# Block attention in half as many TensorE blocks: four heads' scores into four banks, four heads' outputs into one, transposes a piece later

## The chip, the cores and the metric

One core of one Trainium2 chip runs the whole program. The metric is device time in microseconds (us) of that core: the kernel before has a median of 471.4 us over 3 runs (471.27 to 472.64).

## What is computed

A decoder block on 256 tokens of width 1024, all in float32. Three token mixers run on the same normed input: block attention (8 heads of 64), retention (4 heads of 128) and attention on a memory of 256 tokens (4 heads of 128). Their outputs are gated and added, and a feed-forward part with a short convolution follows. With 256 tokens there is a single block of 256, so the block attention is plain causal attention with a relative bias:

```
s_own = einsum('bhqd,bhnd->bhqn', q_c, k_own) * dh**-0.5 + table[:, rel_bucket(d_own)]
s_own = where(d_own >= 0, s_own, NEG_INF)
p     = softmax(s_own)
y     = einsum('bhqn,bhne->bhqe', p, v_own)
```

## The kernel before

All weights stream through in 150 **pieces** of 128x1024. For piece q, SyncE has loaded the raw weights, ScalarE rounds them to a high part `whi` (L141) and VectorE subtracts to get the low part `wlo` (L142); both are made three pieces ahead of their use (`LA = 3`). TensorE then multiplies the piece. A `proj_a` piece is 24 matmuls of 256 columns at L183, a `proj_b` piece is 12 of 512 columns at L170 to L172. A `proj_a` piece goes through its eight k in an order (function `unit`) whose last two matmuls read the low part of the activations for k = 6 and k = 7.

Everything that is not a projection hangs in the gaps between pieces. `at(p, fn, ...)` puts a step on a list, and `tick()` issues the steps of piece p right behind the matmuls of piece p, in the order in which they were listed. Nothing reorders them afterwards: each engine runs its instructions in the order of issue.

The block attention has these steps, at pieces counted from 16:

- `moba_s`: scores. One call takes the two heads that share one 128-partition slice of `qa` and `ka` (64 partitions each), writes them to the two `sps` banks (L370), and has VectorE add the bias and take the two row maxima for both heads (L373, L376).
- `moba_e`: exponentials and row sums on ScalarE (L383).
- `moba_n`: reciprocal and scaling on VectorE (L389, L391).
- `moba_t`: three transposes on TensorE into a `tps` bank (L395 to L397), copied out by ScalarE (L398).
- `moba_v`: outputs of two heads (L409), into one half of the single `yps` bank.
- `moba_y`: rounding and splitting of a full `yps` bank into `ya` (`split_to`: ScalarE L156, VectorE L157), once for every four heads.

For the pair f the scores are issued at piece 16 + 3f, `moba_e` one and two pieces later for its two heads, `moba_n` two and three, `moba_t` three and four, `moba_v` five. Each step is written as one float32 matmul in the source and is two instructions on TensorE.

Other work in the same gaps: the second normed input `nm` (the memory) is split into high and low parts by `Norm.split` at pieces 16 to 19, two k for each piece (`gained`: ScalarE L214, VectorE L215), and is read by the projections of pieces 20 to 27. The projections of pieces 16 to 19 are evacuated into `qm` (L156, L157), those of pieces 20 to 23 into `km`, of 24 to 27 into `vm`, and from piece 28 the retention's `qr` and `kr` are made with rotary products on VectorE (L505, L507). The memory attention starts at piece 30 with the same kinds of banks: `mem_s` (L443) takes an `sps` bank at pieces 30, 33, 36 and 39, `mem_t` (L470) a `tps` bank three pieces later, and `mem_v` (L480) the `yps` bank from piece 34 on.

Of the eight accumulator banks, three are `mm` (projections), two `sps`, two `tps` and one `yps`. All small SBUF tiles (`w2`) share eight buffers.

Of the kernel before, what the change touches and what calls it, by code (L numbers as in the profile page):

```python
# [25 lines left out]
FT = mybir.dt.float32  # L26
FR = mybir.dt.float32r
AF = mybir.ActivationFunctionType
OP = mybir.AluOpType
AX = mybir.AxisListType  # L30

P = 128
D = 1024
T = 256
# [22 lines left out]
def block_kernel(ctx, tc, w, xt, mt, par, cst, onehot, relb, gng, gfin, out):  # L57
    nc = tc.nc
# [4 lines left out]
    act = pool("act")  # L63
# [10 lines left out]
    def s_ps():  # L74
        return psp.tile([P, 512], FT, name="sps", bufs=2)

    def t_ps():
        return psp.tile([P, 512], FT, name="tps", bufs=2)

    def y_ps():  # L80
        return psp.tile([P, 512], FT, name="yps", bufs=1)
# [10 lines left out]
    def w2():  # L92
        return act.tile([P, 512], FT, name="w2", bufs=8)

    def qk_tile():
        return mix.tile([P, 4, T], FT, name="qk", bufs=2)

    def v_tile():
        return mix.tile([P, 2, 512], FT, name="vv", bufs=2)
# [16 lines left out]
    def at(p, fn, *args):  # L116

        works[p].append((fn, args))
# [146 lines left out]
    for k in range(KD):  # L265
        if k < 2 or k % 2 == 0:
            a = 8 + T * k if k else 0
            b = 8 + T * (k + 1 if k < 2 else k + 2)
            nc.sync.dma_start(xs[:, a:b], xt[:, a:b])
        wk, a = (w0, w1)[k // 4], 512 * (k % 4)  # L270
# [55 lines left out]
    hank = mix.tile([P, 8, 384], FT, name="hank")  # L326
# [22 lines left out]
    qa, ka, va = qk_tile(), qk_tile(), v_tile()  # L349
# [9 lines left out]
    asc = 64 ** -0.5  # L359
    mo = {}  # L360
    halves = ((1, slice(0, 256)), (0, slice(256, 384)))

    def moba_s(f):


        sps = [s_ps(), s_ps()]
        for q, k, o in ((slice(128, 256), 256, 0), (slice(0, 128), 128, 256)):
            for hh in range(2):
                pp = slice(64 * hh, 64 * hh + 64)
                nc.tensor.matmul(sps[hh][:, o:o + k], qa[pp, f, q], ka[pp, f, :k], start=True, stop=True)  # L370
        for hh in range(2):
            h, sp, sb = 2 * f + hh, sps[hh], w2()
            nc.vector.scalar_tensor_tensor(sb[:, :384], sp[:, :384], asc, hank[:, h, ::-1], op0=OP.mult, op1=OP.add)  # L373
            mx = act.tile([P, 2], FT, name="amx", bufs=2)
            for t, s in halves:
                nc.vector.tensor_reduce(out=mx[:, t:t + 1], in_=sb[:, s], axis=AX.X, op=OP.max, negate=True)  # L376
            mo["p", h] = sb, mx

    def moba_e(h):
        sb, mx = mo["p", h]  # L380
# [17 lines left out]
        nc.scalar.copy(pt[:, :384], tp[:, :384])  # L398
        mo["t", h] = pt

    def moba_v(f):
        if f % 2 == 0:
            mo["y"] = y_ps()
        o = T * (f % 2)
        for j, a in enumerate((0, 128)):
            for hh in range(2):
                h = 2 * f + hh
                src = mo["t", h][:, 0:256] if j == 0 else mo["t", h][:, 256:384]
                nc.tensor.matmul(mo["y"][64 * hh:64 * hh + 64, o + a:o + 256], va[:, j, 64 * h:64 * h + 64],  # L409
                                 src, start=(j == 0), stop=(j == 1))  # L410

    def moba_y(i):
        split_to(ya, slice(2 * i, 2 * i + 2), kt(mo["y"]))

    for f in range(4):
        b = 16 + 3 * f
        at(b + 5, moba_v, f)
        if f % 2 == 1:
            at(b + 6, moba_y, f // 2)
        at(b, moba_s, f)  # L420
        for hh in range(2):
            at(b + hh + 3, moba_t, 2 * f + hh)
            at(b + hh + 2, moba_n, 2 * f + hh)
            at(b + hh + 1, moba_e, 2 * f + hh)


    qm, km = yt_tile(), yt_tile()
# [58 lines left out]
    for h in range(4):  # L486
        b = 30 + 3 * h
# [147 lines left out]
    for u in range(4):  # L635
        ps = proj_a(mh, 2)
        s = slice(2 * u, 2 * u + 2)
# [51 lines left out]
    for f in range(NF):  # L689
        ps = proj_a(hg if f < DEFER else nh.out)  # L690
        p = count["used"]
        if f < DEFER:
# [4 lines left out]
            p = U0 + 7 + 10 * f  # L697
# [184 lines left out]
```

## Time and profile before

| | |
|---|---|
| median of 3 runs | 471.4 us (471.27 to 472.64) |
| profiled execution | 471.54 us, its span 469.8 us |
| TensorE matmuls busy | 460.1 us, 98% of the span |
| TensorE weight loads busy | 435.7 us, 93% |
| VectorE busy | 348.7 us, 74% |
| ScalarE busy | 258.1 us, 55% |
| GpSimd busy | 61.8 us, 13% |
| DMA | 86.75 MB, mean 185 GB/s |
| mean granted TensorE clock | 0.997 of full speed |

The span runs from the first to the last instruction of the program. Matmuls are pipelined, so one that is said to take 0.28 us is followed by the next after less than half of that; steps from start to start tell more than durations. The block attention lies between 58.9 us and 109.9 us of the span.

### The profile page before, as it was taken

The page shows a single profiled execution, that of the slowest core. Times are in us where ns is not written, and L with a number is a line of the kernel's source. Part 1 is how long each engine was busy: PE and PEld are TensorE (multiplying, and loading weights), DVE is VectorE, ACT ScalarE, POOL GpSimd, SP SyncE. Part 2 cuts the span into 40 slices and gives each one's busy share as a digit, 9 for nine tenths or more (in the row PEclk, how much of TensorE's full clock was granted, in tenths as well). Part 3 has the DMA queues.
Part 4 walks back from the last instruction along what each step waited for, and adds up shares of the span by engine and source line. Part 5 has one row for each costly group of instructions (what it writes and reads, how often), then busy time and mean ns, then how long its engine had stood idle before and what let it go on. Part 6 is the DMA issues. An engine that isn't in the chain of part 4 may idle for free.

```text
span 469.8 us, 8509 instructions
## 1 busy us (share of the span) xinstructions
PE 460.1 (98%) x3470; PEld 435.7 (93%) x3470; DVE 348.7 (74%) x536; ACT 258.1 (55%) x412; POOL 61.8 (13%) x47
## 2 busy tenths in 40 slices
PE   8999999999999999999999999999999999999994
PEld 6899889889989999999999999999999999888883
DVE  5969798768976567776677779989879899744433
ACT  5747575555447434344455656767667676533323
POOL 3354510003210022321000005000000000000003
PEclk9999999999999999999999999999999999999998
DMA  8989744443554445444554574655555545655102
GB/s 259 403 347 309 248 134 162 153 158 134 177 182 140 153 160 179 148 170 166 191 215 145 191 291 161 246 190 176 183 179 180 181 181 179 191 193 196 48 1 89
DMA packets 16342, 86.75 MB, mean 185 GB/s; under 512 B 1672, under 2 KB 4272, under 8 KB 6832
## 3 DMA queue, kind: packets, MB, share of 16 engines
q1 hardware_dynamic: 16016, 85.70, 51.4%
q8 instruction: 27, 0.44, 0.4%
q10 hardware_dynamic: 288, 0.52, 0.3%
q14 instruction: 11, 0.09, 0.1%
HBM read 85.15 MB, written 1.06 MB: 184 GB/s over the span
## 4 chain that ended last, share of the span: by engine, by line
PE 91%; DVE 3%; DMA 1%; issue 1%; SPq 1%; ACT 1%; POOL 0%; POOLq 0%; ACTq 0%; DVEq 0%
PE mm L183 65%; PE mm L172 3%; PE mm L170 3%; PE mm L171 3%; PE tps L710 2%; PE tps L711 2%; PE tps L712 2%; PE sps L710 1%; PE sps L711 1%; PE sps L712 1%; DVE wlo L142 1%; DMA raw<-in_w 1%; DVE act L215 1%; PE yps L409 1%; PE sps L443 1%
## 5 line engine op out<-in xcount | busy, mean ns | idle before, releaser
L183 PE MATMUL mm<-act,whi 128*128 128x256 f32 x1600 | 291.7, 282 | 0.0
L183 PEld LDWEIGHTS mm<-act,whi 128*128 128x128 f32 x1600 | 247.9, 188 | 1.5 <-issue 1.0
L142 DVE TENSOR_TENSOR wlo<-raw,whi 128x1024 fp32r<-128x1024 f32 (+1 forms) x154 | 196.2, 1278 | 65.9 <-ACT whi L141 65.7
L141 ACT CAST whi<-raw 128x1024 fp32r<-128x1024 f32 (+1 forms) x154 | 157.7, 1026 | 123.9 <-PE mm L183 74.5
L183 PE MATMUL mm<-act,wlo 128*128 128x256 f32 x800 | 215.4, 280 | 0.0
L183 PEld LDWEIGHTS mm<-act,wlo 128*128 128x128 f32 x800 | 150.6, 188 | 0.0
L678 DVE SCALAR_TENSOR_TENSOR w<-mm,pr,w 128x255 f32<-128x255 f32 (+1 forms) x72 | 29.8, 478 | 10.2 <-ACT w L673 10.2
L183 PE MATMUL mm<-yt,whi 128*128 128x256 f32 x192 | 36.6, 282 | 0.0
L183 PEld LDWEIGHTS mm<-yt,whi 128*128 128x128 f32 x192 | 30.4, 188 | 0.0
L673 ACT ACTIVATE w<-mm,pr 128x256 f32<-128x256 f32 x36 | 18.4, 560 | 16.3 <-PE mm L183 16.2
L170 PE MATMUL mm<-whi,act 128*128 128x512 f32 x64 | 26.6, 415 | 0.7 <-ACT whi L141 0.7
L172 PE MATMUL mm<-wlo,act 128*128 128x512 f32 x64 | 26.1, 408 | 0.6 <-DVE wlo L142 0.5
L171 PE MATMUL mm<-whi,act 128*128 128x512 f32 x64 | 25.9, 404 | 0.0
L183 PE MATMUL mm<-yt,wlo 128*128 128x256 f32 x96 | 25.1, 282 | 0.0
L739 POOL TENSOR_TENSOR hN<-hN,gfb 128x512 f32<-128x512 f32 x2 | 2.6, 1280 | 169.8 <-ACT w L735 169.8
L183 PEld LDWEIGHTS mm<-yt,wlo 128*128 128x128 f32 x96 | 18.1, 188 | 0.0
L710 PE MATMUL tps<-whi,ah 128*128 128x512 f32 x44 | 17.5, 397 | 0.0
L509 POOL TENSOR_TENSOR qk<-qk,w 128x512 f32<-128x512 f32 x4 | 9.3, 2314 | 62.3 <-DVE w L507 62.3
L711 PE MATMUL tps<-whi,ah 128*128 128x512 f32 x44 | 17.4, 396 | 0.0
L712 PE MATMUL tps<-wlo,ah 128*128 128x512 f32 x44 | 17.3, 393 | 0.0
L172 PEld LDWEIGHTS mm<-wlo,act 128*128 128x128 f32 x64 | 12.3, 192 | 5.2 <-DVE wlo L142 2.5
L170 PEld LDWEIGHTS mm<-whi,act 128*128 128x128 f32 x64 | 12.4, 194 | 3.6 <-ACT whi L141 1.0
(160 smaller groups left out, 504.3 us busy)
## 6 DMA issues: line engine op xcount, KB each, us to landing
raw<-in_w SPq DMA_DIRECT2D x72, 1024.0 KB, 4.9
raw<-in_w SPq DMA_DIRECT2D x8, 256.0 KB, 5.9
raw<-in_w SPq DMA_DIRECT2D x2, 512.0 KB, 6.2
big<-in_mt SPq DMA_DIRECT2D x1, 1024.0 KB
hank<-rel_d SPq DMA_DIRECT2D x1, 1024.0 KB, 12.4
raw<-in_xt SPq DMA_DIRECT2D x1, 1024.0 KB, 4.8
ct<-in_cst SPq DMA_DIRECT2D x1, 770.0 KB, 4.6
big<-in_xt SPq DMA_DIRECT2D x3, 256.0 KB, 5.9
```

The costliest lines, as they stand in the source:

```text
L141: nc.scalar.copy(hi[:, a:b], r)
L142: nc.vector.tensor_tensor(out=lo[:, a:b], in0=r, in1=hi[:, a:b].bitcast(FT), op=OP.subtract)
L170: nc.tensor.matmul(ps[t], xh, wh, start=(k == 0), stop=False)
L171: nc.tensor.matmul(ps[t], xl, wh, start=False, stop=False)
L172: nc.tensor.matmul(ps[t], xh, wl, start=False, stop=(k == KD - 1))
L183: nc.tensor.matmul(p, wk, src[:, b, k], start=(i == 0), stop=(i == len(order) - 1))
L509: nc.gpsimd.tensor_tensor(out=d, in0=d, in1=tmp, op=OP.add)
L673: nc.scalar.activation(ac[:, i], ps[:, i], AF.Identity, bias=pr[:, CONV_B + c:CONV_B + c + 1], scale=cw(2, c))
L678: nc.vector.scalar_tensor_tensor(ac[:, i, s:], ps[:, i, :T - s], cw(2 - s, c), ac[:, i, s:], op0=OP.mult, op1=OP.add)
L710: nc.tensor.matmul(p, xh, hi[:, a:b], start=(f == 0), stop=False)
L711: nc.tensor.matmul(p, xl, hi[:, a:b], start=False, stop=False)
L712: nc.tensor.matmul(p, xh, lo[:, a:b], start=False, stop=(f == NF - 1))
```

## The change

The scores are taken four heads at a time. `moba_s(i)` writes four banks, the two `sps` and the two `tps`, and holds matmuls only; the bias and the maxima become a step of their own for each head, `moba_b`, issued at four pieces one after the other. Outputs are also taken four heads at a time, so `moba_v(i)` fills the whole `yps` bank in one go. There are two calls of each in place of four, at pieces 16 and 24 (scores) and 24 and 32 (outputs). The transposes of a head are issued two pieces behind its `moba_n`, where they were one behind. The buffers `amx` of the maxima go from two to four.

```diff
-    def moba_s(f):
-        sps = [s_ps(), s_ps()]
-        for q, k, o in ((slice(128, 256), 256, 0), (slice(0, 128), 128, 256)):
-            for hh in range(2):
-                pp = slice(64 * hh, 64 * hh + 64)
-                nc.tensor.matmul(sps[hh][:, o:o + k], qa[pp, f, q], ka[pp, f, :k], start=True, stop=True)
-        for hh in range(2):
-            h, sp, sb = 2 * f + hh, sps[hh], w2()
-            nc.vector.scalar_tensor_tensor(sb[:, :384], sp[:, :384], asc, hank[:, h, ::-1], op0=OP.mult, op1=OP.add)
-            mx = act.tile([P, 2], FT, name="amx", bufs=2)
-            for t, s in halves:
-                nc.vector.tensor_reduce(out=mx[:, t:t + 1], in_=sb[:, s], axis=AX.X, op=OP.max, negate=True)
-            mo["p", h] = sb, mx
+    def moba_s(i):
+        mo["s"] = sps = [s_ps(), s_ps(), t_ps(), t_ps()]
+        for f in range(2):
+            for q, k, o in ((slice(128, 256), 256, 0), (slice(0, 128), 128, 256)):
+                for hh in range(2):
+                    pp = slice(64 * hh, 64 * hh + 64)
+                    nc.tensor.matmul(sps[2 * f + hh][:, o:o + k], qa[pp, 2 * i + f, q], ka[pp, 2 * i + f, :k],
+                                     start=True, stop=True)
+
+    def moba_b(h):
+        sp, sb = mo["s"][h % 4], w2()
+        nc.vector.scalar_tensor_tensor(sb[:, :384], sp[:, :384], asc, hank[:, h, ::-1], op0=OP.mult, op1=OP.add)
+        mx = act.tile([P, 2], FT, name="amx", bufs=4)
+        for t, s in halves:
+            nc.vector.tensor_reduce(out=mx[:, t:t + 1], in_=sb[:, s], axis=AX.X, op=OP.max, negate=True)
+        mo["p", h] = sb, mx
...
-    def moba_v(f):
-        if f % 2 == 0:
-            mo["y"] = y_ps()
-        o = T * (f % 2)
-        for j, a in enumerate((0, 128)):
-            for hh in range(2):
-                h = 2 * f + hh
-                ...
+    def moba_v(i):
+        mo["y"] = y_ps()
+        for f in range(2):
+            o = T * f
+            for j, a in enumerate((0, 128)):
+                for hh in range(2):
+                    h = 4 * i + 2 * f + hh
+                    ...
...
-    for f in range(4):
-        b = 16 + 3 * f
-        at(b + 5, moba_v, f)
-        if f % 2 == 1:
-            at(b + 6, moba_y, f // 2)
-        at(b, moba_s, f)
-        for hh in range(2):
-            at(b + hh + 3, moba_t, 2 * f + hh)
-            at(b + hh + 2, moba_n, 2 * f + hh)
-            at(b + hh + 1, moba_e, 2 * f + hh)
+    for i in range(2):
+        b = 16 + 8 * i
+        at(b, moba_s, i)
+        at(b + 8, moba_v, i)
+        at(b + 9, moba_y, i)
+        for j in range(4):
+            at(b + 4 + j, moba_t, 4 * i + j)
+            at(b + 2 + j, moba_n, 4 * i + j)
+            at(b + 1 + j, moba_e, 4 * i + j)
+            at(b + j, moba_b, 4 * i + j)
```

## Rows read from the trace of the kernel before

**Rows 1.** The page: busy time by engine, and the granted TensorE clock in 40 slices.

```profile
PE 460.1 (98%) x3470; PEld 435.7 (93%) x3470; DVE 348.7 (74%) x536; ACT 258.1 (55%) x412; POOL 61.8 (13%) x47
...
PEclk9999999999999999999999999999999999999998
```

**Rows 2.** Busy us by engine, clock, DMA share, GB/s, in the attention's stretch and the next.

```profile
56.00:112.00 56.00, 55.42 (x419) 49.59 (x418) 44.16 (x85) 34.26 (x75) 7.17 (x4) 1.00 0.42 149
112.00:200.00 88.00, 88.00 (x703) 85.71 (x702) 64.11 (x106) 40.35 (x60) 17.16 (x10) 1.00 0.46 161
```

**Rows 3.** Timeline of TensorE around the first score block: start us, us, instruction, count.

```profile
58.60 0.40 PE L183 MATMUL mm<-act,whi 128*128 128x256 f32 x2
58.93 0.92 PE L370 MATMUL sps<-qk 64*128 64x256 f32 x8
59.78 0.50 PE L183 MATMUL mm<-act,whi 128*128 128x256 f32 x2
60.12 0.28 PE L183 MATMUL mm<-act,wlo 128*128 128x256 f32 x1
```

**Rows 4.** Timelines of three narrow windows within that block: its second, third, fourth pair.

```profile
59.25 0.38 PE L370 MATMUL sps<-qk 64*128 64x256 f32 x2
...
59.47 0.39 PE L370 MATMUL sps<-qk 64*128 64x128 f32 x4
...
59.58 0.28 PE L370 MATMUL sps<-qk 64*128 64x128 f32 x2
```

**Rows 5.** Timeline of TensorE around the first output block, then two windows within it.

```profile
76.25 0.40 PE L183 MATMUL mm<-act,whi 128*128 128x256 f32 x2
76.58 0.87 PE L409 MATMUL yps<-w,vv 128*64 128x256 f32 x8
77.38 0.51 PE L183 MATMUL mm<-act,whi 128*128 128x256 f32 x2
77.72 0.28 PE L183 MATMUL mm<-act,wlo 128*128 128x256 f32 x1
...
76.84 0.39 PE L409 MATMUL yps<-w,vv 128*64 128x256 f32 x2
...
77.17 0.28 PE L409 MATMUL yps<-w,vv 128*64 128x128 f32 x2
```

**Rows 6.** Timeline of TensorE from the end of piece 19 to the end of piece 20.

```profile
68.10 0.40 PE L183 MATMUL mm<-act,whi 128*128 128x256 f32 x2
69.08 0.30 PE L395 MATMUL tps<-ct,w 128*128 128x128 f32 x1 [0.58 <-DVE w L391]
...
69.53 0.92 PE L370 MATMUL sps<-qk 64*128 64x256 f32 x8
70.38 0.51 PE L183 MATMUL mm<-act,whi 128*128 128x256 f32 x2
...
73.10 0.40 PE L183 MATMUL mm<-act,whi 128*128 128x256 f32 x2
```

**Rows 7.** Timeline of VectorE in the same stretch.

```profile
61.52 0.55 DVE L373 SCALAR_TENSOR_TENSOR w<-sps,hank 128x384 f32<-128x384 f32 x1
...
68.38 0.55 DVE L391 TENSOR_SCALAR w<-w,ari 128x256 f32<-128x256 f32 x2
68.84 1.22 DVE L142 TENSOR_TENSOR wlo<-raw,whi 128x1024 fp32r<-128x1024 f32 x1
69.98 0.87 DVE L215 SCALAR_TENSOR_TENSOR act<-w,pr,act 128x256 fp32r<-128x256 f32 x2
70.77 0.16 DVE L389 RECIPROCAL ari<-asm 128x2 f32<-128x2 f32 x1
...
71.43 0.55 DVE L373 SCALAR_TENSOR_TENSOR w<-sps,hank 128x384 f32<-128x384 f32 x1
...
72.55 0.55 DVE L373 SCALAR_TENSOR_TENSOR w<-sps,hank 128x384 f32<-128x384 f32 x1
```

**Rows 8.** The tile view of yps: engine, instruction, count, ns min/median/max, first and last start.

```profile
L157 DVE TENSOR_TENSOR yt<-yps,yt x4: 682/684/685, 90.8 to 155.7; 128x512 fp32r<-128x512 f32 x4
```

More of the change, by code (lines that the diff above doesn't have):

```diff
@@ L399, in moba_t @@
         mo["t", h] = pt
-    def moba_v(f):
-        if f % 2 == 0:
-            mo["y"] = y_ps()
-        o = T * (f % 2)
-        for j, a in enumerate((0, 128)):
-            for hh in range(2):
-                h = 2 * f + hh
-                src = mo["t", h][:, 0:256] if j == 0 else mo["t", h][:, 256:384]
-                nc.tensor.matmul(mo["y"][64 * hh:64 * hh + 64, o + a:o + 256], va[:, j, 64 * h:64 * h + 64],
-                                 src, start=(j == 0), stop=(j == 1))
+    def moba_v(i):
[5 more added lines that the diff above has]
+                    h = 4 * i + 2 * f + hh
+                    src = mo["t", h][:, 0:256] if j == 0 else mo["t", h][:, 256:384]
+                    nc.tensor.matmul(mo["y"][64 * hh:64 * hh + 64, o + a:o + 256], va[:, j, 64 * h:64 * h + 64],
+                                     src, start=(j == 0), stop=(j == 1))
     def moba_y(i):
         split_to(ya, slice(2 * i, 2 * i + 2), kt(mo["y"]))
-    for f in range(4):
-        b = 16 + 3 * f
-        at(b + 5, moba_v, f)
-        if f % 2 == 1:
-            at(b + 6, moba_y, f // 2)
-        at(b, moba_s, f)
-        for hh in range(2):
-            at(b + hh + 3, moba_t, 2 * f + hh)
-            at(b + hh + 2, moba_n, 2 * f + hh)
-            at(b + hh + 1, moba_e, 2 * f + hh)
+    for i in range(2):
[8 more added lines that the diff above has]
+            at(b + j, moba_b, 4 * i + j)
     qm, km = yt_tile(), yt_tile()
```

## The prediction, made before the changed kernel was built or run

> **What bounds the kernel now.** I read the page first, for the engine that limits: TensorE's matmuls are busy for 98% of the span and the granted clock is full, 2.4 GHz, in nearly every slice [rows 1]. VectorE has 74%, ScalarE 55%. Then the busy time by stretches, to see whether that average holds where the change is: in the 56 us with the block attention TensorE has 55.42, VectorE 44.16 and ScalarE 34.26 us, and behind it TensorE is busy without a break [rows 2]. So the kernel ends when TensorE has worked through its queue, and time is won only by taking TensorE's own steps away, or a place where it stands still. Whatever is won at 60 to 110 us is kept, since nothing behind it waits for anything but TensorE [rows 2].
>
> Third, the timeline of TensorE by starts, because recorded durations overlap. In a projection matmuls of 256 columns start 0.118 us apart: in piece 20 the second starts at 70.38 + 0.51 - 0.28 = 70.61 and the last, 22 steps later, at 73.10 + 0.40 - 0.28 = 73.22 [rows 6]. Around a score block this pace breaks. The last matmul ahead of it starts at 58.60 + 0.40 - 0.28 = 58.72, the third behind it at 60.12, which is 1.40 us; three steps of the pace would be 0.35, so the block costs **1.05 us** [rows 3]. Inside it the eight instructions run as four pairs, the two heads of a pair together. Second to fourth pair take 59.58 - 59.25 = 0.33 us [rows 4], which is one pass of 256 and one of 128 columns; two of each make 0.66 us of streaming. The other **0.39 us** are lost at entry and exit: the first pair comes 0.09 us late (58.93 against 58.84), the second pair 0.32 us behind it where 0.22 would do, and the first two matmuls behind the block start at 59.78 and 60.00, where 59.69 and 59.81 would be the pace [rows 3, 4]. The output block is the same: 77.72 - 76.37 - 0.35 = **1.00 us**, of which 0.66 stream (77.17 - 76.84 = 0.33 for two passes) and **0.34** are lost [rows 5]. There are four blocks of each kind.
>
> Fourth, idle time. In the whole attention TensorE stands still once: the first transposes, at the end of piece 19, start at 69.08, where the pace would give 68.22 + 0.12 = 68.34 [rows 6]. They wait for the scaling of head 0, which VectorE ends at 68.38 + 0.55 = 68.93 [rows 7]. So **0.74 us** are lost, and from VectorE's result to TensorE's start pass 0.15 us.
>
> **What the change does, part by part.**
>
> *Half as many blocks.* The number of instructions stays, 32 for the scores and 32 for the outputs. A block of 16 pays entry and exit once. If the second half only streams, each merge saves 0.39 (scores) or 0.34 (outputs): 2 x 0.39 + 2 x 0.34 = 1.46 us. The trace has no block of 16. The bounds: a second half that costs as much as a block of its own, 1.05 and 1.00, saves nothing; one that only streams saves 1.46. I take 1.46, because from the second pair on a pair follows the other at streaming pace [rows 4], and the change from the fourth pair to a fifth is of the same kind.
>
> *Outputs directly ahead of scores.* At piece 24 the first output block is followed at once by the second score block. Before, each of the two returned to projections first: second matmul behind it 0.11 late, next entry 0.09 late [rows 3]. Without the return I take 0.20 us off; bounds 0 and, if the whole lead-in of the second block went, 0.39.
>
> *Transposes a piece later.* The scaling of head 0 is now followed by two pieces ahead of its transposes. Up to the end of that scaling VectorE has the same instructions as before in another order (bias steps of heads 0 and 1, three splits, two `wlo`, one `qm` evacuation), so it still ends at 68.93. The transposes come behind piece 20, which can't end before 68.34 + 2.83 = 71.2. The 0.74 us are gone, and there is 2 us of slack. The later heads follow with the same two pieces each. What this hides behind: pieces 20 to 23 of TensorE, 2.8 us each.
>
> *What is late next.* VectorE now takes the bias step of head 2 right behind the scaling of head 0, where before it took it at 71.43. That step is 72.55 - 71.43 = 1.12 us [rows 7]. Queued behind it are the `wlo` that started at 68.84 and the last split of the memory input, done before at 69.98 + 0.87 = 70.85; now 71.97, and with 0.15 us to TensorE 72.12. TensorE wants the two low parts of that split (k = 6 and 7) in the last two matmuls of piece 20. Before, these started at 73.10 and 73.22, 2.3 us behind the split [rows 6, 7]. Now piece 20 has no transposes, no wait and no score block ahead of it: it starts at 68.34 plus the 0.66 us by which the first score block is longer, 69.00, and its last matmul would be at 69.00 + 23 x 0.118 = 71.71. TensorE stands still for 72.12 - 71.71 = **0.41 us**. Bounds: 0, if the longer block takes as much more as a block of its own (then the matmul is due at 72.10), and 1.06, if one more scaling step (70.77 to 71.43, 0.66 us [rows 7]) slips ahead on VectorE.
>
> *What costs nothing.* `moba_b` has the instructions that were in `moba_s`; they run on VectorE beside the pieces. Over pieces 24 to 27 its load is four `wlo` of 1.14 us, four bias steps of 1.12, two scalings of 0.66, and four evacuations of 0.68 [rows 8], 13.1 us against 11.3 us of pieces and 3 us of blocks; so it keeps up, and its leftover is worked off in pieces 28 and 29, where there are no bias steps. Weights are split three pieces ahead, 8.5 us of cover. The two `tps` banks now hold scores until the bias steps of heads 2 and 3 have read them. By the order above the first of these reads ends at 68.93 + 0.55 = 69.5, and the bank's next transposes are due at about 72; the second ends near 73.1, due at 75.3: over 2 us of slack. The `yps` bank is read at piece 33 and wanted again by the memory attention at piece 34, a piece of 2.8 us later, with a rounding on ScalarE and a subtraction of 0.68 us on VectorE to do [rows 8]. More `amx` buffers only remove waits. No DMA is added or moved, and SP's and POOL's queues keep their order.
>
> **The sum.** -1.46 - 0.20 - 0.74 + 0.41 = -1.99 us. Against the profiled execution's 471.54 us (the median, 471.4, is 0.14 lower) that gives 469.55; I forecast **469.5 us**, with 468.7 to 470.0 for this case.
>
> **The rivals.**
>
> *The loss grows with the block.* Entry and exit might be paid for each instruction, or each bank released, and not once a block. For: a block of eight is the only size in the trace. Against: the losses sit at the first pair and behind the last [rows 3, 4], and none is in the middle. Then merging saves nothing, the longer first block delays piece 20 to where the split is in time (wait about 0), and -0.20 - 0.74 remain: 470.6 us. Chance 0.20.
>
> The Trainium skill has a rule that speaks for this side: its page "TensorE: Matmul & The Clock Gate", section "The cost: per-tile semaphore tail", gives the tail of a packed group as about 25 + 4.7 ns for each tile + 26.3 ns for each semaphore increment. By it 8 tiles with two increments have an estimated tail of 115 ns and 16 with four 205 ns, so a merge saves 0.025 us, four save 0.1, and the whole sum would be about -1.0 us, 470.5. The rows show more loss than such a tail, at entry too, and no row here splits it by increments.
>
> *VectorE's backlog takes the place of the old wait.* Piece 20 waits by its upper bound or a second piece waits too: 1.06 in place of 0.41 and as much again at one later place. For: VectorE ran without a gap from 61.52 to 72.55 [rows 7]. Against: over pieces 20 to 23 no bias steps are left. Time: 469.55 + 0.65 to + 1.3, about 470.5 us. Chance 0.16.
>
> *Slower: the transposes' banks.* Scores and transposes share the two `tps` banks; if VectorE reaches the bias steps of heads 2, 3, 6 and 7 late, TensorE stands in order behind the transposes that want the banks, and all pieces behind it. It decides from the point where the reads come 2.2 us later than worked out. To lose the 2 us of gain and 1.4 more, the four waits must add up to 3.4 us, so each read would have to be about 3 us later than worked out. VectorE's order gives no such delay unless its steps lengthen. Time: 473 us. Chance 0.07.
>
> **Range and chances.** The first case has 0.57. What a measurement of this kernel can tell from no change is about 0.3%, 1.4 us: faster means below 470.0. Faster 0.56 (nearly all of the first case), same 0.37 (the two middle ones and the upper end of the first), slower 0.07. The range from 468.7 to 471.2 holds the first case and most of the two middle ones.
>
> **What would show it.** Around the new score block L370 x16, the third projection matmul behind it should start about 0.35 + 1.05 + 0.66 = 2.06 us behind the last one ahead; if 2.45, the first rival holds. The same at L409 with 2.01. At the first transposes there should be no idle time put down to L391. Near the end of piece 20 an idle time of some 0.4 us before L183, put down to VectorE's L215; if it is 0, the split was in time; if over 1, VectorE's backlog is larger than worked out. No idle before L395 put down to L373. What would make the forecast wrong: a second half of a block that does not stream, or a wait at pieces 24 to 34 that this working did not find.

## The result and the profile after

The changed kernel takes **468.55 us** (median of 4 runs, 467.99 to 469.38) against 471.38 us: a ratio of 0.9936, 95% interval 0.9924 to 0.9949. It is 2.8 us faster where 2.0 were forecast (469.5 us), and its median lies 0.15 us under the range.

The page after: busy time by engine.

```profile
PE 457.1 (98%) x3470; PEld 434.8 (93%) x3470; DVE 348.6 (75%) x536; ACT 259.3 (56%) x412; POOL 61.1 (13%) x47
```

The number of instructions is the same as in [rows 1]; TensorE's busy time is 3 us less, and it is still 98% of the span. So TensorE still bounds the kernel, with less time for the same instructions.

TensorE's timeline around the first score block, which answers to [rows 3], and the second output block, which answers to [rows 5]:

```profile
58.89 0.40 PE L183 MATMUL mm<-act,whi 128*128 128x256 f32 x2
59.22 0.92 PE L371 MATMUL sps<-qk 64*128 64x256 f32 x8
59.98 0.82 PE L371 MATMUL tps<-qk 64*128 64x256 f32 x8
60.73 0.51 PE L183 MATMUL mm<-act,whi 128*128 128x256 f32 x2
61.07 0.28 PE L183 MATMUL mm<-act,wlo 128*128 128x256 f32 x1
...
112.67 0.39 PE L183 MATMUL mm<-act,whi 128*128 128x256 f32 x2
113.00 1.52 PE L413 MATMUL yps<-w,vv 128*64 128x256 f32 x16
114.45 0.51 PE L183 MATMUL mm<-act,whi 128*128 128x256 f32 x2
114.80 0.28 PE L183 MATMUL mm<-act,wlo 128*128 128x256 f32 x1
```

From the last matmul ahead (58.89 + 0.40 - 0.28 = 59.01) to the third behind (61.07) it is 2.06 us; less 0.35 for three steps, the block of 16 costs 1.71, which is 1.05 + 0.66. The output block: 114.80 - 112.78 - 0.35 = 1.67, which is 1.00 + 0.67. So the second half only streams.

At piece 24, outputs and scores are back to back:

```profile
84.93 0.39 PE L172 MATMUL mm<-wlo,act 128*128 128x512 f32 x1
85.25 1.52 PE L413 MATMUL yps<-w,vv 128*64 128x256 f32 x16
86.70 0.92 PE L371 MATMUL sps<-qk 64*128 64x256 f32 x8
87.46 0.82 PE L371 MATMUL tps<-qk 64*128 64x256 f32 x8
88.21 0.50 PE L170 MATMUL mm<-whi,act 128*128 128x512 f32 x1
88.55 0.39 PE L171 MATMUL mm<-whi,act 128*128 128x512 f32 x1
88.78 0.40 PE L172 MATMUL mm<-wlo,act 128*128 128x512 f32 x1
```

Here the steps are 0.234 us (512 columns), so the pair of blocks costs 88.78 - 84.93 - 0.70 = 3.15 us, 0.23 less than 1.71 + 1.67.

The end of piece 20, which answers to [rows 6], and VectorE there, which answers to [rows 7]:

```profile
71.75 0.28 PE L183 MATMUL mm<-act,wlo 128*128 128x256 f32 x1
71.89 0.79 PE L183 MATMUL mm<-act,whi 128*128 128x256 f32 x2
72.52 0.27 PE L398 MATMUL tps<-ct,w 128*128 128x128 f32 x1
```

```profile
68.65 0.55 DVE L394 TENSOR_SCALAR w<-w,ari 128x256 f32<-128x256 f32 x2
69.11 0.55 DVE L376 SCALAR_TENSOR_TENSOR w<-tps,hank 128x384 f32<-128x384 f32 x1
...
70.23 1.22 DVE L142 TENSOR_TENSOR wlo<-raw,whi 128x1024 fp32r<-128x1024 f32 x1
71.36 0.88 DVE L215 SCALAR_TENSOR_TENSOR act<-w,pr,act 128x256 fp32r<-128x256 f32 x2
```

The transposes no longer wait: the scaling ends at 69.20, they start at 72.52. The last two matmuls of piece 20 do wait for the split that VectorE ends at 72.24. The first starts at 71.89, the second not 0.12 but 0.40 us later (71.89 + 0.79 - 0.38 = 72.29, with 0.38 the duration of a first one after a stop), and the transposes 0.23 behind it. In the steps 71.75 to 72.52 TensorE takes 0.77 us for three steps of 0.12: 0.42 us are lost.

Everything so far is as forecast. To see where the rest comes from, the same three landmarks (starts of a piece that both kernels have) are read in both traces: the first matmul of piece 16, of piece 36 (attention and the pieces around it lie between) and of piece 86 (long runs of projections lie between). First the kernel before, then after:

```profile
55.99 0.41 PE L183 MATMUL mm<-act,whi 128*128 128x256 f32 x2
126.57 0.40 PE L170 MATMUL mm<-whi,act 128*128 128x512 f32 x1
280.38 0.48 PE L183 MATMUL mm<-act,whi 128*128 128x256 f32 x2
```

```profile
56.27 0.41 PE L183 MATMUL mm<-act,whi 128*128 128x256 f32 x2
124.96 0.40 PE L170 MATMUL mm<-whi,act 128*128 128x512 f32 x1
277.54 0.48 PE L183 MATMUL mm<-act,whi 128*128 128x256 f32 x2
```

| | 16 to 36 | 36 to 86 | 86 to the end |
|---|---|---|---|
| before | 70.58 | 153.81 | 189.37 |
| after | 68.69 | 152.58 | 189.21 |
| difference | -1.89 | **-1.23** | -0.16 |

The part with the attention gives 1.89 us. Another 1.23 us come from pieces 36 to 86, where no work was added, moved or taken away. No idle time of TensorE goes there: from 112 to 200 us it is busy for 88.00 of 88 us before [rows 2], and after:

```profile
112.00:200.00 88.00, 88.00 (x706) 85.12 (x705) 62.50 (x104) 40.65 (x57) 17.12 (x11) 1.00 0.43 156
```

What differs is the step, the time from the start of one matmul to the start of the next. The view by windows counts TensorE's matmuls in one stretch of 55 us, before and then after:

```profile
215.00:270.00 55.00, 55.00 (x464) 1.00 0.53 184
```

```profile
215.00:270.00 55.00, 55.00 (x471) 1.00 0.51 183
```

A matmul is counted if any of its 0.28 us lies in the window, so 55.28 us hold 464 or 471: a mean step of 119.1 ns against 117.4 ns, at the same granted clock, 2.4 GHz.

Pieces 76 to 85 show it in ten pieces that read nothing but `act`, `whi` and `wlo`. Piece 76 starts here, before and after:

```profile
251.54 0.40 PE L183 MATMUL mm<-act,whi 128*128 128x256 f32 x2
```

```profile
249.02 0.40 PE L183 MATMUL mm<-act,whi 128*128 128x256 f32 x2
```

Up to piece 86 it is 28.84 us before and 28.52 after, for the same 240 matmuls.

### The profile page after: what moved, and what is told of

Same layout as the page of the kernel before. It is cut to its first block, busy times and chain, and to the rows that moved or that the text cites. A ratio compares the mean times of both kernels' runs of the same rounds, so it can differ in the third digit from the quotient of the medians.

```text
span 466.8 us, 8507 instructions
## 1 busy us (share of the span) xinstructions
PE 457.1 (98%) x3470; PEld 434.8 (93%) x3470; DVE 348.6 (75%) x536; ACT 259.3 (56%) x412; POOL 61.1 (13%) x47
## 4 chain that ended last, share of the span: by engine, by line
PE 94%; DMA 2%; DVE 1%; ACT 0%; SPq 0%; POOL 0%; issue 0%; POOLq 0%; ACTq 0%; DVEq 0%
PE mm L183 68%; PE mm L172 3%; PE mm L170 3%; PE mm L171 3%; DMA raw<-in_w 2%; PE tps L714 2%; PE tps L716 2%; PE tps L715 2%; PE sps L714 1%; PE sps L716 1%; PE sps L715 1%; PE yps L413 1%; PE yps L484 1%; PE sps L447 1%; PE yps L715 0%; PE yps L714 0%
## 5 line engine op out<-in xcount | busy, mean ns | idle before, releaser
L513 POOL TENSOR_TENSOR qk<-qk,w 128x512 f32<-128x512 f32 x4 | 8.2, 2054 | 61.4 <-PE tps L400 45.3
```

What stands on the lines that cost most here:

```text
L513: nc.gpsimd.tensor_tensor(out=d, in0=d, in1=tmp, op=OP.add)
```

## Experiments

Each ratio is against the kernel before as measured in the same round: 471.44 us for e1 to e4, 471.36 for e5 to e8, 471.48 for e9 to e11.

**e1 and e2: both kernels again, no edit.** Is the step fixed by the program, or drawn in each execution?

> The kernel before, unchanged, profiled once more. In its first trace the 256-column matmuls of the long run of projections between 215 and 270 us started 119.0 ns apart, in the changed kernel's trace 117.3 ns. If the step is fixed by the program, it is 119.0 ns again and the time 471.4 us within 0.3. If the step is drawn anew in every execution, it can be 117.3 ns here, and the time then about 470.3 us.

> The changed kernel, unchanged, profiled once more. If the step is fixed by the program: 117.3 ns between 215 and 270 us, and 468.5 us within 0.3. If it is drawn anew: it may be 118.7 or more, with 469.5 us or above. The waits and blocks of the attention itself (one stop of about 0.3 us at the end of piece 20) should be the same in either case.

Measured: 471.51 us (ratio 0.9999, interval 0.9989 to 1.0008) and 468.15 us (0.9926, interval 0.9912 to 0.9941). The three stretches are 70.57, 153.81, 189.38 us and 68.64, 152.58, 189.24 us, to 0.05 us those of the first traces. From piece 40 on each piece of 256-column matmuls has the same step in both executions of a program, to 0.1 ns, so there it is fixed by the program. Before that it is not: in piece 28 the fourth matmul and the last, 20 steps apart, start at 100.113 and 102.486 us in the first trace of the kernel before (118.7 ns) and at 100.182 and 102.529 us in e1 (117.4 ns).

**e3: transposes a piece later, alone**, in the kernel before.

```diff
-        at(b + 5, moba_v, f)
+        at(b + 6, moba_v, f)
...
-            at(b + 6, moba_y, f // 2)
+            at(b + 7, moba_y, f // 2)
...
-            at(b + hh + 3, moba_t, 2 * f + hh)
+            at(b + hh + 4, moba_t, 2 * f + hh)
```

> The kernel before with the transposes, outputs and their splitting one piece later and nothing else; the blocks stay four and four. Both theories: the stop of 0.74 us ahead of the first transposes goes, the memory input's split is in time, so the end of the attention comes 0.74 us earlier. If that is all, 470.65 us. If the step of the later projections changes with where the attention ends, the time can differ from this by up to 1.3 us with no new wait in the trace.

Measured: 470.50 us, 0.9977 (0.9968 to 0.9987). Stretches: 69.38, 153.83, 189.40 us. TensorE's timeline at the end of piece 19 has no stop:

```profile
68.08 0.40 PE L183 MATMUL mm<-act,whi 128*128 128x256 f32 x2
68.41 0.92 PE L370 MATMUL sps<-qk 64*128 64x256 f32 x8
69.27 0.51 PE L183 MATMUL mm<-act,whi 128*128 128x256 f32 x2
```

The attention's stretch is 1.20 us shorter, more than the 0.74: with outputs one piece later, two output blocks now stand directly ahead of a score block (pieces 22 and 25), and each such pair saves some 0.2 us, as at piece 24 of the changed kernel. The later stretches are those of the kernel before, to 0.03 us: moving the work does not move the step.

**e4: score blocks of 16 cut into two of 8**, in the changed kernel.

```diff
...
-        at(b, moba_s, i)
+        at(b, moba_s, i, 0)
+        at(b + 1, moba_s, i, 1)
```

The first call writes the `sps` banks (heads 0 and 1 of the four), the second the `tps` banks (heads 2 and 3).

> The changed kernel with the score blocks of 16 cut into two of 8, the second one piece later; outputs and transposes as changed. If entry and exit are paid once a block: two more entries, +0.78 us, less the 0.3 us stop at piece 20 that then goes, so the attention ends 0.4 to 0.5 us later than in the changed kernel and the time is 469.0 us if the step of the later projections stays. If the loss grows with the instructions of a block: no loss, 468.3 us.

Measured: 468.79 us, 0.9939 (0.9922 to 0.9955); stretches 69.10, 152.58, 189.21. The second of the small blocks:

```profile
62.53 0.39 PE L183 MATMUL mm<-act,whi 128*128 128x256 f32 x2
62.85 0.92 PE L372 MATMUL tps<-qk 64*128 64x256 f32 x8
63.70 0.50 PE L183 MATMUL mm<-act,whi 128*128 128x256 f32 x2
64.04 0.28 PE L183 MATMUL mm<-act,wlo 128*128 128x256 f32 x1
```

64.04 - 62.64 - 0.35 = 1.05 us: a block of 8 costs what it cost before, with entry and exit of its own. The attention's stretch is 0.41 us longer than in the changed kernel, inside the expected 0.4 to 0.5; the stop at piece 20 is gone with it. The medians (0.24 and 0.64 us above the two of the changed kernel) can't tell this well; the stretches can.

**e7: output blocks of 16 cut into two of 8**, in the changed kernel.

```diff
...
-        at(b + 8, moba_v, i)
+        at(b + 6, moba_v, i, 0)
+        at(b + 8, moba_v, i, 1)
```

> The changed kernel with the output blocks of 16 cut into two of 8, the first two pieces earlier. If entry and exit are paid once a block: 0.34 us more for each of two, 469.0 us, the second half still directly ahead of the scores at piece 24. If the loss grows with a block's instructions: 468.4 us.

Measured: 468.99 us, 0.9946 (0.9931 to 0.9961); stretches 69.20, 152.57, 189.25. The attention's stretch grows by 0.51 us where 0.68 was expected: the sign and most of the size of a loss paid once a block. The first halves now stand directly ahead of transposes:

```profile
78.78 0.39 PE L183 MATMUL mm<-act,whi 128*128 128x256 f32 x2
79.10 0.87 PE L413 MATMUL yps<-w,vv 128*64 128x256 f32 x8
...
80.53 0.28 PE L183 MATMUL mm<-act,wlo 128*128 128x256 f32 x1
```

From 78.89 to 80.53, less 0.35, the two cost 1.29 us, where such a block and three transposes apart from each other cost 1.00 and 0.33 (in e8 from 71.43 to 72.11, less 0.35). Two such places give some 0.1 of the missing 0.17 us; the rest stays open.

**e5: the kernel before with four `amx` buffers**, and nothing else. It is a line of the change that the prediction set at nothing. It issues the same instructions in the same order; what is allocated behind `amx` (the tiles `pt`, `vv`, `hank`, `qk`, `yt`, `gnb`, `hN`, `gfb`, `ah` among them) lies 64 bytes a partition higher. The weights `whi` and `wlo` and the activations `act16` (`act` in the rows) are allocated ahead of it and stay where they were.

```diff
-            mx = act.tile([P, 2], FT, name="amx", bufs=2)
+            mx = act.tile([P, 2], FT, name="amx", bufs=4)
```

> The kernel before with four buffers for the row maxima (amx) in place of two, and no other edit: no instruction is added, removed or moved, only the addresses of what is allocated behind them shift by two small tiles. If the step of the later projections hangs on where the tiles lie: 117.3 ns between 215 and 270 us as in the changed kernel, and about 470.3 us. If it hangs on the order of the instructions or on where the attention ends: 118.7 to 120.2 ns as before, and 471.4 us.

**e6: the changed kernel with two `amx` buffers**, the reverse edit.

> The changed kernel with two amx buffers in place of four, no other edit. If the step hangs on where the tiles lie: 118.7 to 120.2 ns between 215 and 270 us as before, and 469.4 us, which is what the prediction's sum gave. If on the instructions: 117.3 ns and 468.4 us.

Measured: e5 470.09 us, 0.9974 (0.9964 to 0.9983), and e6 469.91 us, 0.9966 (0.9953 to 0.9979). The window counts, e5 and then e6:

```profile
215.00:270.00 55.00, 55.00 (x471) 1.00 0.53 182
```

```profile
215.00:270.00 55.00, 55.00 (x465) 1.00 0.51 182
```

And the landmarks of e6:

```profile
55.88 0.41 PE L183 MATMUL mm<-act,whi 128*128 128x256 f32 x2
124.48 0.40 PE L170 MATMUL mm<-whi,act 128*128 128x512 f32 x1
278.29 0.48 PE L183 MATMUL mm<-act,whi 128*128 128x256 f32 x2
```

The stretches of e5 are 70.61, 152.57, 189.23 us: the attention as before, the rest as after. (Its profiled execution took 471.41 us, the longest of its ten: piece 16 started at 57.22 us there, 1.23 later than in the kernel before, which the stretches leave out.) Those of e6 are 68.60, 153.81, 189.38 us: the attention as after, the rest as before. The two parts of the change come apart cleanly: the work on the attention makes 1.9 to 2.0 us, the two small buffers some 1.4. Of the 2.8 us measured, about half is therefore luck: the kernel before had a slow layout of its tiles, and the edit happened to leave it.

**e9, e10, e11: other layouts**, in the kernel before. Which tile's place matters?

```diff
+    pad = mix.tile([P, 16], FT, name="pad")
+    nc.vector.memset(pad, 0.0)
     ya = yt_tile()
```

This is e9: 64 bytes ahead of `yt`, with nothing else moved but `gnb`.

```diff
-            mx = act.tile([P, 2], FT, name="amx", bufs=2)
+            mx = act.tile([P, 2], FT, name="amx", bufs=6)
```

This is e10, a shift of 128 bytes; e11 has `bufs=3`, a shift of 32 bytes.

> The kernel before with an unused tile of 64 bytes a partition put ahead of the yt tiles (one tiny VectorE memset writes it), so that of all matmul operands only the four yt tiles lie 64 bytes higher. If the matmul step hangs on where yt lies, since yt is the moving operand of every third piece from 42 to 75: 117.3 ns between 215 and 270 us and about 470.2 us. If another shifted tile matters (pt, vv, qk, ah): 118.7 to 120.2 ns and 471.4 us.

> The kernel before with six amx buffers: the shift is 128 bytes a partition. If what counts is the place of yt modulo 128 bytes, it is as in the kernel before: 118.7 to 120.2 ns and 471.4 us. If any shift, or the smaller number of waits with more buffers, does it: 117.3 ns and 470.2 us.

> The kernel before with three amx buffers: the shift is 32 bytes a partition. If yt must lie at a multiple of 64 bytes or less, or if the number of buffers does it: 117.3 ns, 470.2 us. If it must lie at a multiple of 128 bytes: a slower step, 118.7 ns or more, and 471.4 us or a little above.

| | shift, bytes | time, us | ratio and interval | 36 to 86 | 86 to the end |
|---|---|---|---|---|---|
| before | 0 | 471.38 | | 153.81 | 189.37 |
| e9 | yt alone, 64 | 471.11 | 0.9989 (0.9979 to 0.9998) | 153.33 | 189.41 |
| e11 | 32 | 470.66 | 0.9978 (0.9969 to 0.9988) | 153.09 | 189.19 |
| e10 | 128 | 470.33 | 0.9971 (0.9959 to 0.9982) | 152.85 | 189.19 |
| e5 | 64 | 470.09 | 0.9974 (0.9964 to 0.9983) | 152.57 | 189.23 |

My theory, that the place of `yt` modulo 128 bytes decides, fell twice: `yt` alone gives 0.48 of the 1.23 us, and 128 bytes give 0.96. Nor is it the number of buffers: e9 changes the stretch with two, and six give less than four. Each layout has a value of its own between 152.6 and 153.8 us, and the kernel before happened to have the longest of the five.

**e8: head 2's bias step behind the split**, in the changed kernel, to take away the new stop.

```diff
+        if i == 0:
+            at(b + 3, moba_b, 2)
         for j in range(4):
...
-            at(b + j, moba_b, 4 * i + j)
+            if (i, j) != (0, 2):
+                at(b + j, moba_b, 4 * i + j)
```

> The changed kernel with the bias step of head 2 issued one piece later, at piece 19 behind the last split of the memory input instead of ahead of it. If VectorE's order makes the stop at the end of piece 20: it goes, 0.28 us less, 468.1 us. If the stop comes from something else (ScalarE's high part, or the longer score block): it stays, 468.4 us.

VectorE and TensorE at the end of piece 20:

```profile
68.56 1.22 DVE L142 TENSOR_TENSOR wlo<-raw,whi 128x1024 fp32r<-128x1024 f32 x1
69.70 0.88 DVE L215 SCALAR_TENSOR_TENSOR act<-w,pr,act 128x256 fp32r<-128x256 f32 x2
70.49 0.55 DVE L376 SCALAR_TENSOR_TENSOR w<-tps,hank 128x384 f32<-128x384 f32 x1
```

```profile
71.31 0.40 PE L183 MATMUL mm<-act,whi 128*128 128x256 f32 x2
71.54 0.27 PE L398 MATMUL tps<-ct,w 128*128 128x128 f32 x1
```

Measured: **467.53 us**, 0.9918 (0.9903 to 0.9933), the fastest kernel of the study. The split now ends at 70.58, ahead of the matmuls that read it, and the transposes follow at the normal step. The attention's stretch is 68.19 us, 0.50 less than in the changed kernel (0.28 was expected: I had counted the stop without the late start behind it, 0.42 together; the other 0.08 is little more than the 0.05 between two executions). The other two stretches are those of the changed kernel. The interval of the ratio overlaps with that of the changed kernel; the stretch is what shows the gain.

## Why the prediction was wrong

**Half as many blocks: right.** 1.71 and 1.67 us for blocks of 16, against 1.71 and 1.66 in the sum. e4 gives the loss back.

**Outputs directly ahead of scores: right.** 0.23 us against 0.20.

**Transposes a piece later: right.** The 0.74 us are gone, also when it is done alone (e3).

**What is late next: right in place and cause, in size partly by luck.** 0.42 us against 0.41, behind VectorE's split, and gone when the bias step of head 2 is moved behind it (e8). But the 0.42 are a stop of 0.28 and a start of the transposes 0.11 us late (0.23 behind the last matmul, 0.11 in e8). The working had no such late start, and 0.15 us from VectorE's result to TensorE's start where 0.05 were seen (72.24 to 72.29); the two errors cancel.

Together these are four output blocks at 1.00, four score blocks at 1.05 replaced by 1.71 + 1.67 + 3.15, that is -1.67, then -0.74 and +0.42: -1.99 us, the forecast's sum. The stretch shows -1.89, and e6, which has these edits alone, -1.98. By its median e6 is 1.45 us below the kernel before (469.91 against 471.36; by the interval 0.99 to 2.22), so the stretch is what confirms the size.

**The step that failed** is in "What costs nothing": "More `amx` buffers only remove waits." The term was set at nothing. The buffers removed no wait that counted: the attention's stretch in e5 is that of the kernel before (70.61 against 70.58). They moved what lies behind them by 64 bytes, and the steps of TensorE in pieces 36 to 86 and later fell, worth 1.23 + 0.16 us (e5, e6). With them the sum is -1.99 - 1.39 = -3.4 us; the profiled execution was 3.0 us shorter, of which 0.28 went the other way in a later start of piece 16 (56.27 against 55.99). Underneath is an assumption of the first part, that TensorE's time changes only with the instructions it has and the places where it stands still. The step itself, 0.118 us throughout in my working, is a third way, and the trace of the kernel before already had more than one: 117.4 ns in piece 30 (fourth matmul at 106.436, last at 108.783 us) and 120.0 in piece 50 (173.243 and 175.643).

**The rivals.** *The loss grows with the block*: fell, since a block of 16 lost no more than one of 8. The rule of the Trainium skill that stood beside it ("TensorE: Matmul & The Clock Gate", section "The cost: per-tile semaphore tail") made an estimated 0.025 us of a merge; the rows show 0.39 and 0.33, so the measurement decides. *VectorE's backlog*: came only as the one stop. *The transposes' banks*: VectorE's read of the first shared bank ended at 69.66, 2.9 us ahead of the transposes at 72.52, and no wait of TensorE is put down to the bias step.

**What stays open.** Which tile's place sets the step, and through what, is not settled: moving `yt` (and `gnb`) alone changes it, moving more tiles changes it further, but no rule over the five layouts was found. It is not only the place of what a matmul reads: pieces 76 to 85 read `act`, `whi` and `wlo`, which no layout moved, and take 28.84 us in the kernel before and e6, 28.52 in the changed kernel and e5. Why pieces follow a layout whose moved tiles they do not read was not tried. Moving one tile at a time by 32, 64 and 128 bytes was not tried either.

## What to carry to other kernels

Where TensorE works without gaps, count what a block in another shape loses at entry and exit (here 0.34 to 0.39 us with 8 instructions or 16), and merge blocks or set them side by side. After removing a wait, follow the engine that was waited for to the next thing queued behind the step that you moved. An edit of a few bytes in a buffer's size is not free of effect: time it alone before a gain of half a per cent is put down to the idea, and compare stretches between landmarks, which here agreed to 0.05 us between two executions, where the medians of the changed kernel differ by 0.4.

## What was not expected of the hardware

The same matmuls at the same granted clock (2.4 GHz) have different steps. Most pieces of 256 columns keep one of 117.4, 118.7 and 120.0 ns from end to end. From piece 40 on, which one follows the layout of the tiles in memory: every piece has the same step in all programs of one layout (the kernel before, e1, e3 and e6; the changed kernel, e2, e4, e5, e7 and e8), although pieces 16 to 36 take from 68.19 to 70.61 us in them. Before piece 40 it also changes from one execution to the next. That pieces change whose own operands did not move (76 to 85) is what nothing here explains. The page "TensorE: Matmul & The Clock Gate" of the Trainium skill, section "Back-to-back issue gap", gives 262 cycles for an isolated matmul of 256 columns at full clock, an estimated 109 ns, and says that in a stream of weight loads and matmuls both set the spacing. The steps here are 8 to 11 ns longer than that gap, and no run tells which share the weight loads have.
